# A 192-byte pad under the gate and up weight parts, and another order of the row blocks in the last output-projection column

## The chip, the core and the metric

One NeuronCore of a Trainium2 chip runs the whole kernel. The metric is the device time of one execution in microseconds (us). Between engines the kernel is told by these names: PE is TensorE's matmul stream and PEld its weight loads, DVE is VectorE, ACT is ScalarE, POOL is GpSimd, SP is SyncE, which here only issues DMAs.

## What is computed

One layer of a hybrid block on 512 positions of width 2048, all in float32, and a final RMSNorm:

```python
h = rmsnorm(x, norm1_gain[l])
proj = h @ w_in[l]
o_a = hgrn2_mixer(q_a, f_a, i_a, g_a, lb_all[l], hgrn_norm_gain[l])
o_b = fox_mixer(q_b, k_b, v_b, f_b, fox_gate_bias[l])
x = x + jnp.concatenate([o_a, o_b], axis=-1) @ w_out[l]
h = rmsnorm(x, norm2_gain[l])
x = x + conv_ffn(h, w_ffn_gate[l], w_ffn_up[l], ffn_conv_w[l], ffn_conv_b[l], w_ffn_down[l])
return rmsnorm(x, final_norm_gain)
```

`conv_ffn` multiplies `h` by a gate and an up matrix of 2048 x 5632, passes the gate branch through a causal convolution of width 3 and SiLU, multiplies it with the up branch, and projects back to 2048.

## The kernel before

**Products in parts.** Every float32 product is made of three float32r matmuls: each operand is split into a high part (an ACT copy to float32r) and a low part (a DVE subtraction), and high x high, low x high and high x low are added up in PSUM. That is lines 218 to 220 for the projections and lines 850 to 852 for gate and up.

**Stages.** The input projections, the two mixers, the output projection (columns `d` of 128, each a sum over 16 row blocks `k`, lines 763 to 770), gate and up together (44 blocks `f` in `glu`, line 861), the down projection, the final norm. In the output projection a tile `os_[k]` holds the two parts of row block `k` of the mixers' output, two tiles of 2048 bytes per partition each, in the pool `pa`. All 16 columns read all 16 blocks; the last column (`d` = 15) reads them in the order `LASTK` (line 768), and the host lays its weights out in that order (line 1058).

**The gate and up stage.** The two matrices of a block `f` go through a fast scheme of seven products of half size (`ORDER`, line 785, `NAMES`, line 705) instead of eight. The weights arrive from HBM in tiles `wq` of 4096 bytes per partition (pool `wf`, eight of them, lines 788 to 797), SP issues the loads and POOL those that add to a tile while they land. ACT and DVE split each into `fhi` and `flo` (pool `wh`, four of each, lines 832 to 835). A product is 8 x 3 matmuls with the weight part as stationary operand and a 128x256 piece of the normalised activations (the forms `b11`, `n1`, `b21`, `n2`, `b22`, `n4`, `t3`) as moving operand; 44 x 7 x 24 = 7392 matmuls.

**The passage between them.** After the last column `pa` and the weight stream's pools are closed, and `wf` and `wh` open on the same SBUF bytes (lines 771 to 784), and `tl`, which takes the last pieces of the forms. A new tile waits for the last reader of each old tile under it, tile by tile, so a `wq` load waits for the matmul of the last column that reads the row block that lies below it. The last column's result goes through `x1_out` (lines 747 to 761): DVE adds the rows of x that POOL loaded into `xr` (line 749, 750), SP stores the sum (line 751), ACT squares it and scales it into `hg` (lines 245, 754), and ACT and DVE make the last pieces of the forms (lines 716 to 719). A scheduler sets the order of each engine's instructions when the program is built, not the order of the lines: on ACT the first `fhi` (line 834) stands behind the square, `hg` and three forms of the last column.

**The pad.** `shifted(SHIFT)` (lines 73 and 783) takes a tile of `SHIFT` float32 per partition between `wf` and `wh`. All that is allocated above it moves with it: `fhi`, `flo`, and the tiles of `glu` (pool `gt`, line 902). By the addresses of the built program the forms begin at multiples of 512 bytes, and so do the weight parts of the projections; `fhi` and `flo` begin 64 bytes past one.

Of the kernel before, what the change touches and what calls it, by code (L numbers as in the profile page):

```python
# [25 lines left out]
SCALE = 128.0**-0.5  # L26
NEG = -1.0e30
RAW = 1024
LASTK = (4, 5, 3, 6, 0, 1, 7, 2, 8, 9, 10, 11, 12, 13, 14, 15)
PIECE = 512  # L30
NLATE = 4
ND = KT - NLATE
# [7 lines left out]
KP = KT // 2  # L40
FORM = KP * P
LEAD = 2
SHIFT = 16
EVEN = 376
EVEN_CM = 24
EVEN_SM = 40
# [11 lines left out]
def tile_hymba_block(ctx: ExitStack, tc: tile.TileContext, xT, wst, wgu, wdn, wfb, consts, out, out_t):  # L58
# [5 lines left out]
    def opened(name, bufs, side="left", **kw):  # L64
        cm = tc.tile_pool(name=name, bufs=bufs, side=side, reuse_waits="tile", **kw)
        pools[name] = (cm, cm.__enter__())
        return pools[name][1]
# [5 lines left out]
    def shifted(n):  # L73

        opened("sh", 1).tile([P, n], F32, name="shift")
# [28 lines left out]
    def MM():  # L104
        return mm.tile([P, T], F32, name="mmt", tag="mm")
# [116 lines left out]
    def unit(ps, ks, hs, first=True, last=True):  # L222

        for i, k in enumerate(ks):
            mms(ps, [(k, *ws.block())], hs, first and i == 0, last and i == len(ks) - 1)
            step()
# [539 lines left out]
    for d in range(WOPEN, KT):  # L766
        ps = MM()
        unit(ps, range(KT) if d < KT - 1 else LASTK, os_)
        if d < KT - 1:
# [12 lines left out]
    wf = opened("wf", 8)  # L782
    shifted(SHIFT)
    wh = opened("wh", LEAD + 2)
# [252 lines left out]
def _weights(w_in, w_out, w_gate, w_up, w_down):  # L1037
# [3 lines left out]
    def cols(w, c0, n):  # L1041
        return w[:, c0:c0 + n].reshape(-1, P, n).transpose(1, 0, 2).reshape(P, -1)
# [14 lines left out]
    parts += [cols(w_out, d * P, P) for d in range(WOPEN, KT - 1)]  # L1057
    order = np.concatenate([np.arange(k * P, (k + 1) * P) for k in LASTK])
    parts.append(cols(w_out[order], last, P))
# [50 lines left out]
```

## Time and profile before

| | |
|---|---|
| median of 3 runs | 2238.32 us |
| lowest and highest | 2236.76 and 2239.03 us |
| profiled execution | 2237.23 us |
| its span, first to last instruction | 2235.5 us |
| time around the span | 1.73 us |
| PE busy | 2217.3 us, 99% of the span, 13662 matmuls |
| PEld, DVE, ACT, POOL busy | 1975.1, 1449.0, 947.3, 148.2 us |
| mean granted TensorE clock | 0.997 of full |

A row of the timeline gives the start in us from the span's start, the duration, engine, line, operation, tiles as out<-in, shape, and in brackets how long the engine stood idle before it and what ended that. Equal neighbours are merged into one row with their count. Matmuls are pipelined: the duration of one is longer than the distance from its start to the next one's, and it is the distance that adds up to time.

### The profile page before, as it was taken

How to read it: one execution, taken by the hardware profiler on the slowest of the kernel's cores; microseconds unless marked ns; L12 is line 12 of the kernel's file. 1: busy time of each engine (PE TensorE's matmuls, PEld its weight loads, DVE VectorE, ACT ScalarE, POOL GpSimd, SP SyncE). 2: the span in 40 equal slices, each digit the busy share in tenths (PEclk: the TensorE clock that was granted, in tenths of full speed). 3: DMA queues.
4: the chain of work that ended last, by engine and by line, in shares of the span. 5: the costliest groups of instructions: out<-in, count | busy, mean ns of one | idle time of the engine just before them, and what ended most of it. 6: DMA issues, size and time to landing. Idle time of an engine off the chain costs nothing.

```text
span 2235.5 us, 34427 instructions
## 1 busy us (share of the span) xinstructions
PE 2217.3 (99%) x13662; PEld 1975.1 (88%) x13662; DVE 1449.0 (65%) x2210; ACT 947.3 (42%) x1528; POOL 148.2 (7%) x243
## 2 busy tenths in 40 slices
PE   9999999999999999999999999999999999999998
PEld 8888888788888887999999999999999888888886
DVE  6666467646457464888888888888888433333345
ACT  6333233234335454555555555555555222222334
POOL 0000000000000000100000000000002402010000
PEclk9999999999999999999999999999999999999999
DMA  5222322222222354788888888888887935242233
GB/s 192 85 76 86 99 71 98 76 85 76 87 83 78 125 162 145 230 222 219 222 226 227 220 223 224 224 220 218 223 221 201 377 114 199 94 172 101 87 102 113
DMA packets 112066, 352.14 MB, mean 158 GB/s; under 512 B 12800, under 2 KB 19072, under 8 KB 111904
## 3 DMA queue, kind: packets, MB, share of 16 engines
q1 hardware_dynamic: 89568, 272.67, 36.4%
q0 software_dynamic: 22192, 77.15, 15.5%
q8 instruction: 107, 1.75, 0.3%
q14 instruction: 55, 0.45, 0.1%
q10 hardware_dynamic: 144, 0.12, 0.0%
HBM read 318.43 MB, written 31.46 MB: 157 GB/s over the span
## 4 chain that ended last, share of the span: by engine, by line
PE 98%; DMA 1%; DVE 1%; ACT 0%; issue 0%; DVEq 0%; POOL 0%; ACTq 0%; POOLq 0%
PE pq L850 12%; PE pq L852 12%; PE pq L851 12%; PE mmt L218 9%; PE mmt L220 9%; PE mmt L219 9%; PE mxt L218 7%; PE mxt L219 7%; PE mxt L220 7%; PE mmt L300 3%; PE mmt L302 3%; PE mmt L301 3%; DMA raw<-wdn 0%; PE mxt L452 0%; PE mxt L643 0%; PE mxt L1028 0%
## 5 line engine op out<-in xcount | busy, mean ns | idle before, releaser
L164 DVE TENSOR_TENSOR wlo<-raw,whi 128x512 fp32r<-128x512 f32 x453 | 311.7, 689 | 447.7 <-ACT whi L163 406.6
L163 ACT ACTIVATE whi<-raw 128x512 fp32r<-128x512 f32 x453 | 284.6, 630 | 664.8 <-PE mxt L219 300.4
L835 DVE TENSOR_TENSOR flo<-wq,fhi 128x1024 fp32r<-128x1024 f32 x308 | 376.1, 1222 | 93.4 <-ACT fhi L834 89.7
L834 ACT ACTIVATE fhi<-wq 128x1024 fp32r<-128x1024 f32 x308 | 326.2, 1060 | 236.7 <-issue 105.4
L218 PE MATMUL mmt<-at,whi 128*128 128x512 f32 x896 | 354.7, 396 | 0.0
L220 PE MATMUL mmt<-at,wlo 128*128 128x512 f32 x896 | 349.7, 390 | 0.0
L219 PE MATMUL mmt<-at,whi 128*128 128x512 f32 x896 | 349.3, 390 | 0.0
L218 PE MATMUL mxt<-qt,whi 128*128 128x512 f32 x660 | 256.1, 391 | 1.0 <-ACT whi L163 0.9
L220 PE MATMUL mxt<-qt,wlo 128*128 128x512 f32 x660 | 256.8, 389 | 0.0
L219 PE MATMUL mxt<-qt,whi 128*128 128x512 f32 x660 | 256.5, 389 | 0.0
L220 PEld LDWEIGHTS mmt<-at,wlo 128*128 128x128 f32 x896 | 168.2, 188 | 36.0
L218 PEld LDWEIGHTS mmt<-at,whi 128*128 128x128 f32 x896 | 168.3, 188 | 34.5 <-issue 1.9
L219 PEld LDWEIGHTS mmt<-at,whi 128*128 128x128 f32 x896 | 168.4, 188 | 33.0
L218 PEld LDWEIGHTS mxt<-qt,whi 128*128 128x128 f32 x660 | 123.9, 188 | 27.4 <-ACT whi L163 1.7
L220 PEld LDWEIGHTS mxt<-qt,wlo 128*128 128x128 f32 x660 | 123.9, 188 | 25.9
L219 PEld LDWEIGHTS mxt<-qt,whi 128*128 128x128 f32 x660 | 123.9, 188 | 25.5 <-issue 0.2
L797 POOL DMA_DIRECT2D wq<-wgu x87 | 75.0, 862 | 754.2 <-DMA wq<-wgu 316.3
L818 DVE TENSOR_TENSOR wq<-wq 128x1024 f32<-128x1024 f32 x88 | 107.6, 1222 | 1.5
L850 PE MATMUL pq<-b11h,fhi 128*128 128x256 f32 x352 | 98.3, 279 | 4.1 <-ACT fhi L834 4.1
L300 PE MATMUL mmt<-whi,at 128*128 128x512 f32 x256 | 100.8, 394 | 0.0
L850 PE MATMUL pq<-b21h,fhi 128*128 128x256 f32 x352 | 97.8, 278 | 2.1 <-ACT p L869 2.1
L301 PE MATMUL mmt<-whi,at 128*128 128x512 f32 x256 | 99.7, 390 | 0.0
(304 smaller groups left out, 5033.1 us busy)
## 6 DMA issues: line engine op xcount, KB each, us to landing
wq<-wgu SPq DMA_DIRECT2D x220, 512.0 KB, 5.7
raw<-wst SPq DMA_DIRECT2D x143, 512.0 KB, 3.4
wq<-wgu POOLq DMA_DIRECT2D x87, 512.0 KB, 7.8
raw<-wdn SPq DMA_DIRECT2D x87, 512.0 KB, 3.5
qt<-actd POOLq DMA_DIRECT2D x88, 256.0 KB, 6.9
actd<-ah SPq DMA_DIRECT2D x44, 256.0 KB, 2.9
actd<-al SPq DMA_DIRECT2D x44, 256.0 KB, 5.3
xt<-xT SPq DMA_DIRECT2D x16, 256.0 KB, 5.8
```

The lines of the kernel that those rows point to most:

```text
L163: queue_ends[:] = [s.activation(hi, src, AF.Copy), v.tensor_tensor(lo, src, f32(hi), op=ALU.subtract)]
L164: v.tensor_tensor(lo, src, f32(hi), op=ALU.subtract)]
L218: pe.matmul(ps, lhsT=a, rhs=xh[:, ts], start=(first and i == 0), stop=False)
L219: pe.matmul(ps, lhsT=a, rhs=xl[:, ts], start=False, stop=False)
L220: last_mm[:] = [pe.matmul(ps, lhsT=b, rhs=xh[:, ts], start=False, stop=(last and i == n - 1))]
L300: pe.matmul(pss[i], lhsT=xh[:, ts], rhs=hi, start=(k == 0), stop=False)
L301: pe.matmul(pss[i], lhsT=xl[:, ts], rhs=hi, start=False, stop=False)
L834: s.activation(hi, t, AF.Copy)
L835: v.tensor_tensor(lo, t, f32(hi), op=ALU.subtract)
L850: pe.matmul(ps, lhsT=a, rhs=th, start=(first and j == 0), stop=False, **kw)
L851: pe.matmul(ps, lhsT=a, rhs=tl, start=False, stop=False, **kw)
L852: last_mm[:] = [pe.matmul(ps, lhsT=b, rhs=th, start=False, stop=(j == KP - 1), **kw)]
```

## The change

Two constants are changed and nothing else.

```diff
-LASTK = (4, 5, 3, 6, 0, 1, 7, 2, 8, 9, 10, 11, 12, 13, 14, 15)
+LASTK = (11, 12, 4, 5, 6, 3, 7, 0, 1, 8, 2, 9, 10, 13, 14, 15)
-SHIFT = 16
+SHIFT = 48
```

`SHIFT` counts float32, so the pad grows from 64 to 192 bytes per partition; `fhi`, `flo` and the tiles of `glu` lie 128 bytes higher, and the first `fhi` begins 192 instead of 64 bytes past a multiple of 512. No instruction is added or taken away.

**PE, the last column of the output projection.** `mmt` is the column's sum in PSUM, `whi` and `wlo` the weight parts, and each three rows are one row block: `at_6007` and `at_6008` are the parts of block 11, `at_6014` and `at_6015` those of block 12, `at_5924` and `at_5925` those of block 4.

```order
 L219 MATMUL mmt_7391<-at_6303,whi_7410 128x512
 L220 MATMUL mmt_7391<-at_6302,wlo_7411 128x512
+L218 MATMUL mmt_7469<-at_6007,whi_7428 128x512
+L219 MATMUL mmt_7469<-at_6008,whi_7428 128x512
+L220 MATMUL mmt_7469<-at_6007,wlo_7429 128x512
+L218 MATMUL mmt_7469<-at_6014,whi_7428 128x512
+L219 MATMUL mmt_7469<-at_6015,whi_7428 128x512
+L220 MATMUL mmt_7469<-at_6014,wlo_7429 128x512
 L218 MATMUL mmt_7469<-at_5924,whi_7428 128x512
 L219 MATMUL mmt_7469<-at_5925,whi_7428 128x512
```

Blocks 11 and 12 were the twelfth and thirteenth of the column and are the first two now: 11 blocks, or 33 matmuls, earlier.

**SP, the first loads of the gate and up weights.** `wq` are the eight tiles, `x1d` is the store of column 14's sum; in brackets stand the semaphores that a load waits for, PE_49 being that of the matmuls.

```order
 L751 DMA x1d<-xr 128x512 [waits DMAHW0_49,DVE_49]
+L795 DMA wq<-wgu 128x1024 [waits PE_49] x2
+L795 DMA wq<-wgu 128x1024 [waits DMAHW3_49,PE_49]
 L795 DMA wq<-wgu 128x1024 [waits PE_49]
-L795 DMA wq<-wgu 128x1024
-L795 DMA wq<-wgu 128x1024 [waits DMAHW3_49]
-L795 DMA wq<-wgu 128x1024
-L795 DMA wq<-wgu 128x1024 [waits DMAHW5_49]
-L795 DMA wq<-wgu 128x1024 [waits DMAHW6_49]
-L795 DMA wq<-wgu 128x1024 [waits DMAHW7_49]
-L795 DMA wq<-wgu 128x1024 [waits DMAHW0_49]
```

Before, the first load waited for the matmul of line 219 on block 12, the 38th of the column's 48, and the other seven had nothing of PE left to wait for. Now each of the eight waits for PE by itself: in their order for the 5th, 11th, 14th, 20th, 29th, 35th, 38th and 39th matmul of the column.

**ACT, the passage.** Its order is the same in both programs; this is that of the changed one, from the square of column 15 on.

```order
L245 ACTIVATE sq<-xr 128x512 [waits DVE_49]
L754 ACTIVATE hg<-xr,con 128x512
L717 ACTIVATE b21h_7598<-hg 128x256 [waits Activation_49]
L717 ACTIVATE b22h_7608<-hg 128x256
L717 ACTIVATE n2h_7604<-tq 128x256 [waits DVE_49]
L834 ACTIVATE fhi<-wq 128x1024 [waits DMAHW1_49]
```

The first `fhi` stands behind the five operations of column 15, as before. One wait ahead of these rows has another value: `b11h` of the last pair of columns (line 717) waits for a matmul that stands nine later than before. DVE's order is the same in both programs too.

## Rows read from the trace of the kernel before

**Rows 1.** The page: busy time by engine, and the chain that ended last.

```profile
PE 2217.3 (99%) x13662; PEld 1975.1 (88%) x13662; DVE 1449.0 (65%) x2210; ACT 947.3 (42%) x1528; POOL 148.2 (7%) x243
...
PE 98%; DMA 1%; DVE 1%; ACT 0%; issue 0%; DVEq 0%; POOL 0%; ACTq 0%; POOLq 0%
```

**Rows 2.** Waits of PE: for whom, us in total, times, longest.

```profile
PE pq L850 <- ACT fhi L834: 4.1, 1, 4.1
...
PE pq L850 <- ACT p L869: 2.1, 1, 2.1
...
PE pq L852 <- DVE flo L835: 0.6, 1, 0.6
```

**Rows 3.** Timeline of PE, end of the last column and after.

```profile
887.18 0.39 PE L219 MATMUL mmt<-at,whi 128*128 128x512 f32 x1
...
889.45 0.39 PE L220 MATMUL mmt<-at,wlo 128*128 128x512 f32 x1
893.90 0.58 PE L850 MATMUL pq<-b11h,fhi 128*128 128x256 f32 x1 [4.06 <-ACT fhi L834]
...
899.91 0.28 PE L850 MATMUL pq<-n1h,fhi 128*128 128x256 f32 x1
...
905.44 0.28 PE L852 MATMUL pq<-n2h,flo 128*128 128x256 f32 x1
```

**Rows 4.** Timeline of SP, POOL, DVE and ACT in the passage.

```profile
869.44 0.33 SPq L156 DMA_DIRECT2D raw<-wst  x1
...
879.72 0.33 SPq L751 DMA_DIRECT2D x1d<-xr  x1
...
882.23 0.42 ACT L717 ACTIVATE b11h<-hg 128x256 fp32r<-128x256 f32 x1 [1.26 <-PE mmt L219]
...
882.24 0.54 POOL L749 DMA_DIRECT2D xr<-xT  x1 [10.20 <-DMA x1d<-xr]
...
887.61 12.18 SPq L795 DMA_DIRECT2D wq<-wgu  x9
...
889.88 0.69 DVE L750 TENSOR_TENSOR xr<-xr,mmt 128x512 f32<-128x512 f32 x1 [8.45 <-PE mmt L220]
...
890.60 0.63 ACT L245 ACTIVATE sq<-xr 128x512 f32<-128x512 f32 x1 [0.31 <-DVE xr L750]
...
892.50 0.40 ACT L717 ACTIVATE n2h<-tq 128x256 fp32r<-128x256 f32 x1
892.81 1.04 ACT L834 ACTIVATE fhi<-wq 128x1024 fp32r<-128x1024 f32 x1
...
895.48 0.42 DVE L718 TENSOR_TENSOR t3l<-tq,t3h 128x256 fp32r<-128x256 f32 x1
895.81 1.22 DVE L830 TENSOR_TENSOR wq<-wq 128x1024 f32<-128x1024 f32 x1
```

**Rows 5.** DMA issues at 887.6, 882.2, 871.5 and 899.3 us: size, us to landing.

```profile
wq<-wgu SPq DMA_DIRECT2D x1, 512.0 KB, 3.6
xr<-xT POOLq DMA_DIRECT2D x1, 256.0 KB, 3.1
xr<-xT POOLq DMA_DIRECT2D x1, 256.0 KB, 3.3
wq<-wgu POOLq DMA_DIRECT2D x1, 512.0 KB, 9.4
```

**Rows 6.** Timeline of ACT before PE's second wait.

```profile
905.69 1.06 ACT L834 ACTIVATE fhi<-wq 128x1024 fp32r<-128x1024 f32 x1 [0.61 <-ACT fhi L834]
906.77 1.28 ACT L263 ACT_TABLE_LOAD   x1
908.06 0.20 ACT L263 ACTIVATE sd<-va 128x4 f32<-128x4 f32 x1
908.17 0.37 ACT L869 ACTIVATE p<-pq 128x256 f32<-128x256 f32 x1
```

**Rows 7.** Stretches: start:end, length, PE busy (matmuls), granted clock, DMA share, GB/s.

```profile
892.70:899.60 6.90, 5.11 (x22) 0.51 1.07 406
909.90:913.20 3.30, 3.30 (x18) 0.50 1.02 371
1000.00:1700.00 700.00, 700.00 (x6179) 1.00 0.82 221
```

**Rows 8.** Timeline of PE in the stretch from 909.9 us on.

```profile
910.05 0.41 PE L852 MATMUL pq<-b21h,flo 128*128 128x256 f32 x1
...
912.83 0.41 PE L850 MATMUL pq<-b22h,fhi 128*128 128x256 f32 x1
```

## The prediction

> **What bounds the kernel now.** I read the page first: PE is busy for 2217.3 of 2235.5 us and the chain that ended last runs through PE for 98% of the span [rows 1]. So only two things can move the time: PE's few idle stretches, and the distance from one matmul to the next. The waits of PE are the next view. All of them over half a microsecond in the two stages that the change touches are three: 4.1 us and 0.6 us at the start of the gate and up stage, where the first product waits for `fhi` and then for `flo`, and 2.1 us two products later, for ACT's copy of a sum [rows 2]. From then on the stage runs without a wait; 6179 matmuls in 700.0 us are 0.1133 us from one to the next [rows 7]. The last look is at the passage itself, engine by engine, to see who holds PE there.
>
> PE's last matmul of the output projection starts at 889.45 and ends at 889.84, and the first of the next stage starts at 893.90 [rows 3]. In between DVE adds column 15 to x (889.88), ACT squares the sum (890.60) and goes through `hg` and three forms without a break to 892.50, and the first `fhi` starts at 892.81 [rows 4]. The reader is to see what is missing in that last row: there is no bracket. `fhi` did not wait for its weights; ACT came to it straight from `n2h`. Its load was issued at 887.61 [rows 4] and landed 3.6 us later [rows 5], at 891.2, which is 1.6 us before ACT was free. The same holds for the second product: DVE adds `a22` to `s1` at 895.81, straight after `t3l` [rows 4].
>
> **The new order of row blocks.** No matmul is added, and PE's order inside the column changes nothing for PE, because all 16 blocks are long there. What moves is SP's loads. The matmul that the first load waited for starts at 887.18 [rows 3], and 33 matmuls earlier at 0.227 us each ((889.45 - 887.18) / 10 [rows 3]) makes 7.5 us: the load goes out at about 880.1, right behind the store of column 14 at 879.72 [rows 4]. By the positions in the column the others follow at 881.5, 882.2, 883.5, 885.6, 886.9, 887.6 and 887.8. The first tile lands at about 883.7 instead of 891.2. But the wait that ends last at 893.90 is ACT's, and ACT's order is unchanged: `fhi` still stands behind `n2h`, that behind DVE's sum, and that behind PE's last matmul. Gain: 0. What lies beside the loads is ACT's own chain from 889.88 to 892.81; it covers them now by 1.6 us and after the change by 9 us.
>
> One wait moves the other way: ACT's `b11h`, which started at 882.23 [rows 4], waits for a matmul nine later, 9 x 0.227 = 2.0 us. Behind it on ACT stands only what started at 889.88 and later, so this is hidden by 5 us. Cost: 0.
>
> The second wait does not depend on the loads either. ACT starts an `fhi` at 905.69, 0.25 us after PE started the last matmul of the product before (905.44 [rows 3]), loads a table for 1.28 us, takes a root and copies the sum for 0.37 us [rows 6], and PE goes on. I put the start of that `fhi` down to PE, which still reads the buffer that it writes; the view names ACT's own `fhi` there, which can't be it. Gain: 0.
>
> What could be lost is the row load `xr` for column 15. It starts at 882.24 on POOL, once the store of column 14 has landed, and takes 3.1 us [rows 4, 5], so it lands at 885.3, 4.5 us before DVE needs it at 889.88. Now the first `wq` loads are under way beside it. Nearest row: the same load one column earlier, 2 us behind a 512 KB weight load that SP issued at 869.44, took 3.3 us [rows 4, 5]. Far row: a POOL load behind SP's full queue took 9.4 us [rows 5], and it is twice as large. With 3.3 nothing happens; with 9.4 `xr` would land at 891.6 and the passage would be 1.8 us longer. The loads come at 0.7 to 2.0 us from each other and not eight at once, so I take the near row: cost 0, with 0 to 1.8 us as bounds. A rule speaks against the change here: the Trainium skill (DMA: Bandwidth & Descriptors, Issuing engines are not separate DMA queues) says that DMAs of all issuing engines run on the same 16 engines and interleave. The 9.4 us agree with it, the 3.3 us say how little one neighbour costs. By the rule alone the cost would be the 1.8 us.
>
> **The pad.** `fhi` and `flo` move by 128 bytes. On ACT and DVE that touches no wait of PE after the passage. On PE it could change the distance between matmuls, if weight load and moving operand get in each other's way by their addresses; no row shows a pad of 192. From below: at half the clock the distance is (912.83 - 910.05) / 13 = 0.2138 us [rows 8], half of that is 0.1069, so at full clock 0.0064 us per matmul are something else; were it the pad's, 7392 x 0.0064 = 47 us could go. From above: the 48 matmuls from 899.91 to 905.44 stand (905.44 - 899.91) / 47 = 0.1177 us apart [rows 3], at the same pad; were this the rule in the stage, it would cost 7392 x 0.0044 = 33 us. I take 0. The output projection, whose weight parts have no pad at all, needs 0.227 us for 512 columns [rows 3], and the padded stage 0.1133 for 256 [rows 7]: the same per column, so two placements give one pace, and a third should too.
>
> **The sum** is 0, against the profiled execution's 2237.23 us (span 2235.5 and 1.73 around it). The median of the three runs is 1.1 us above it; carried over, the forecast is **2238.3 us**. A measurement of this kernel tells about 0.2%, 4.5 us, from no change.
>
> **The rivals.**
>
> *The loads were the bound after all (faster, 2231.0 us).* If something in `fhi`'s start hung on the loads, the whole start could go: 4.06 us of wait, and the first product, whose 24 matmuls took 899.91 - 893.90 = 6.0 us [rows 3] for want of `flo` and at a granted clock of 0.51, the lower of its two levels (1.2 GHz), to which it fell while PE stood still [rows 7], where 24 x 0.1133 = 2.7 are due. That is 4.06 + 3.3 = 7.3 us. For it: PE stands still just there, and the loads are what the change moves. Against it: the missing bracket, and 1.6 us of slack. The Trainium skill (DMA: Bandwidth & Descriptors, Rules for kernel authors) says to issue a DMA early, compute, and wait for it late; by that this rival is what one expects, but here the trace has the wait on ACT. 14%.
>
> *The pad costs pace (slower, 2271 us).* The weight reads then fall against the moving operand's so that the slow distance of 0.1177 us becomes the stage's own: +33 us. If only one of the three matmuls of a step suffers it is 11 us, 2249. It decides from 0.0006 us per matmul on (4.5 / 7392). For it: the slow distance exists. Against: it came once, after the first product, and the same buffers run at 0.1133 later. 11%.
>
> *The row load comes late (up to 1.8 us, 2240.1; or more).* The wait grows from 4.06 to 5.9 us, and a longer wait can lengthen the stretch at half the clock, where 18 matmuls took 3.3 us instead of 2.0 [rows 7], 1.3 us each: 1.8 + 2 x 1.3 = 4.4 us with two, and more with a third. 8%, of which 5 lie within 0.2%.
>
> *The pad gains pace (faster, 2191 us).* The 47 us from above. Against it stands the equal pace per column. 5%.
>
> **How the numbers follow.** The forecast has 62%. Within 0.2% lie it and five of the third rival: 0.67. Faster are the first and the last: 0.19. Slower are the second and three of the third: 0.14. The range reaches down to the first rival's 2231 and up over the late row load to 2243; it leaves out both results of the pad, 16%.
>
> **What would show it.** In the changed kernel's timeline SP's first `wq` load stands near 880.1 and the eight are spread to 887.8; `fhi` again starts about 2.9 us after the last matmul's end, with no wait for a DMA; PE waits 4.1, 0.6 and 2.1 us in the same three places; the stretch from 1000 to 1700 us holds 6179 matmuls again, give or take two. A bracket with a DMA at DVE's addition of column 15 would be the third rival. The forecast is wrong if PE's first wait shrinks by more than a microsecond, or if the distance in the long stretch leaves 0.1133.

## The result and the profile after

The changed kernel takes 2269.12 us (median of 4 runs, 2268.60 to 2269.88) against 2238.24 us before (4 runs): 1.0139 times as long, 95% interval 1.0126 to 1.0151. The forecast was 2238.3 us, the range ended at 2243; the rival "the pad costs pace" had 2271. The profiled execution took 2269.88 us, with a span of 2268.2.

PE's waits first, as [rows 2] shows them for before:

```profile
PE pq L850 <- ACT fhi L834: 4.1, 1, 4.1
PE mxt L1017 <- DVE dg L1010: 3.2, 1, 3.2
PE pq L850 <- ACT p L869: 2.1, 1, 2.1
...
PE pq L852 <- DVE flo L835: 0.6, 1, 0.6
```

In the passage and the stage behind it nothing waits longer. The passage, in the order of [rows 4], from the timelines of SP, POOL, DVE and ACT of the changed kernel:

```profile
879.80 0.33 SPq L751 DMA_DIRECT2D x1d<-xr  x1
880.21 19.66 SPq L795 DMA_DIRECT2D wq<-wgu  x9
...
882.47 0.54 POOL L749 DMA_DIRECT2D xr<-xT  x1 [10.33 <-DMA x1d<-xr]
...
884.35 0.42 ACT L717 ACTIVATE b11h<-hg 128x256 fp32r<-128x256 f32 x1 [3.30 <-PE mmt L219]
...
889.96 0.69 DVE L750 TENSOR_TENSOR xr<-xr,mmt 128x512 f32<-128x512 f32 x1 [8.45 <-PE mmt L220]
...
892.58 0.40 ACT L717 ACTIVATE n2h<-tq 128x256 fp32r<-128x256 f32 x1
892.89 1.04 ACT L834 ACTIVATE fhi<-wq 128x1024 fp32r<-128x1024 f32 x1
```

The first load goes out 7.4 us earlier, and `fhi` starts again where ACT is done with `n2h`: 892.89 instead of 892.81. The whole passage stands 0.08 us later, as the column before it already does (the store at 879.80 instead of 879.72), and is no longer and no shorter.

The long stretch is where the time is. The stretches of [rows 7], of the changed kernel (start:end, length, PE busy with its matmuls, granted clock, DMA share, GB/s):

```profile
892.70:899.60 6.90, 5.03 (x25) 0.56 0.98 208
909.90:913.20 3.30, 3.30 (x21) 0.62 0.93 227
1000.00:1700.00 700.00, 700.00 (x5946) 1.00 0.79 213
```

PE is busy for all of the 700 us, at the full clock (2.4 GHz), with 5946 matmuls instead of 6179. That is 0.1177 us from one to the next instead of 0.1133; by their starts, 7272 matmuls from 915.90 to 1772.66, it is 0.1178, the value that the text uses. The last matmul of the stage starts at 1772.66 us instead of 1740.70; less the 0.08 us, that is 31.9 us of the 32.7 by which the span grew. No wait of PE shows any of it; only the count in a stretch does.

The changed kernel also held the fast pace for a while. PE's timeline, from the second product on:

```profile
899.58 0.28 PE L850 MATMUL pq<-n1h,fhi 128*128 128x256 f32 x1
...
905.12 0.28 PE L852 MATMUL pq<-n2h,flo 128*128 128x256 f32 x1
...
908.26 0.39 PE L850 MATMUL pq<-b21h,fhi 128*128 128x256 f32 x1 [2.08 <-ACT p L869]
...
912.49 0.28 PE L851 MATMUL pq<-b21l,fhi 128*128 128x256 f32 x1
...
915.10 0.28 PE L850 MATMUL pq<-b22h,fhi 128*128 128x256 f32 x1
...
915.44 1.02 PE L277 MATMUL mxt<-dg,ones 128*128 128x512 f32 x2
915.90 0.68 PE L850 MATMUL pq<-n4h,fhi 128*128 128x256 f32 x1
```

From 899.58 to 905.12 are 47 distances, 0.1179 us each, and from 912.49 to 915.10 are 23, 0.1135 us each; then comes a float32 matmul of the norm (line 277), and behind it the pace is 0.1178 to the end of the stage. Between the first two stretches lie eight small matmuls of the norm, the wait of 2.1 us, and a stretch at half the clock (1.2 GHz), which began when PE had been going again for 0.7 us:

```profile
909.00:912.40 3.40, 3.40 (x19) 0.50 0.90 263
```

The kernel before does the same up to the matmul of line 277. It has 0.1177 us at first [rows 3], and then

```profile
913.96 0.28 PE L852 MATMUL pq<-b22h,flo 128*128 128x256 f32 x1
...
915.66 0.28 PE L852 MATMUL pq<-b22h,flo 128*128 128x256 f32 x1
915.78 1.02 PE L277 MATMUL mxt<-dg,ones 128*128 128x512 f32 x2
```

15 distances of 0.1133 us. Only behind that matmul do the two kernels part: the one before keeps 0.1133 to the end of the stage, the changed one falls back.

### The profile page after: what moved, and what is told of

Read it like the earlier page. It is cut to its first block, busy times and chain, and to the rows that moved or that the text cites. A ratio compares the mean times of both kernels' runs of the same rounds, so it can differ in the third digit from the quotient of the medians.

```text
span 2268.2 us, 34432 instructions
## 1 busy us (share of the span) xinstructions
PE 2249.1 (99%) x13662; PEld 2006.8 (88%) x13662; DVE 1451.7 (64%) x2210; ACT 950.6 (42%) x1528; POOL 148.3 (7%) x243
## 4 chain that ended last, share of the span: by engine, by line
PE 98%; DMA 1%; DVE 1%; ACT 0%; issue 0%; SPq 0%; DVEq 0%
PE pq L851 13%; PE pq L850 13%; PE pq L852 13%; PE mmt L218 9%; PE mmt L220 9%; PE mmt L219 9%; PE mxt L219 7%; PE mxt L218 7%; PE mxt L220 7%; PE mmt L300 3%; PE mmt L302 2%; PE mmt L301 2%; DMA raw<-wdn 1%; PE mxt L452 0%; PE mxt L643 0%; PE mxt L1028 0%
```

## The experiments

### Which of the two edits

```diff
-SHIFT = 16
+SHIFT = 48
```

> The pad of 192 bytes with the old order of row blocks. Theory A, the pad alone sets the distance between matmuls of the gate and up stage: 0.1178 us through the stage, 2269 us. Theory B, the stage has a fast and a slow pace at any pad, and what happens in the passage (with the new order the half-clock stretches begin 0.9 us earlier) leaves PE in one of them: with the old order the pace is 0.1133 us and the time 2238 us. Theory C, it takes both: 2238 us here and in the run with the order alone.

Measured: 2269.91 us, ratio 1.0145 (1.013 to 1.016), and again 5946 matmuls from 1000 to 1700 us.

```diff
-LASTK = (4, 5, 3, 6, 0, 1, 7, 2, 8, 9, 10, 11, 12, 13, 14, 15)
+LASTK = (11, 12, 4, 5, 6, 3, 7, 0, 1, 8, 2, 9, 10, 13, 14, 15)
```

> The new order of row blocks with the pad of 64 bytes. Theory A: the pace is 0.1133 us, 2238 us, and PE's three waits stay at 4.1, 0.6 and 2.1 us. Theory B: 0.1178 us and 2269 us. Theory C: 2238 us.

Measured: 2237.13 us (10 runs) against 2237.10 (13), ratio 1.0000 (0.9990 to 1.0009), 6179 matmuls. The pad alone gives the whole loss, and the order of the row blocks nothing, as forecast for it. Theories B and C fall as they were put. Both paces occur at either pad, as theory B said, but the order of the row blocks does not choose between them.

### Other pads

No pad (the pool opens without its tile), and `SHIFT` of 32, 8, 12, 24 and 80 (the first two of these edits are shown), each with the old order:

```diff
-    shifted(SHIFT)
+    opened("sh", 1)
```

> Old order, no pad at all: the first weight part begins at a multiple of 512 bytes, as the forms do. Theory A needs one pace for this place and can't say which; by the old projections, whose parts lie at multiples of 512 and run at the same pace per column as the stage with 64 bytes, it is 0.1133 us and 2238 us. Theory B: the timing of the passage is that of before, so 0.1133 us and 2238 us whatever the pad.

```diff
-SHIFT = 16
+SHIFT = 32
```

> Old order, a pad of 128 bytes, between the two. Theory A: one of the two paces through the whole stage, 2238 or 2269 us; if the place within 128 bytes counts, 64 and 192 would have been alike, so a slow pace here would say that larger distances are bad and a fast one that 192 is a place by itself. Theory B: 0.1133 us and 2238 us whatever the pad.

> Old order, pad of 32 bytes, between 0 (0.1200 us) and 64 (0.1133 us). If a step of 64 bytes has to be crossed, the pace is that of no pad, 0.1200 us and 2285 us; if the pace falls with the distance, about 0.1167 us and 2261 us; if any distance of 32 will do, 0.1133 us and 2238 us.

> Old order, pad of 48 bytes. If the pace falls evenly from 32 to 64, 0.1158 us and about 2256 us; if 64 is a narrow place, about 0.118 us and 2272 us; if a good stretch reaches down here, 0.1133 us and 2238 us. A pace under 0.1133 us would say that 17 sixteenths of the columns are no floor.

> Old order, pad of 96 bytes. So far the pace goes by the distance of the weight part from the form, taken modulo 256 bytes: 0 gives 0.1200 us, 32 0.1183, 64 and 320 0.1133, 128 0.1187, 192 0.1178. If 64 is the middle of a good stretch, 96 keeps 0.1133 us and 2238 us; if 64 is a narrow place, it lies near the value of 128: 0.1187 us and 2276 us.

> Old order, pad of 320 bytes, which is 64 more than 256. If places 256 bytes apart are alike, 0.1133 us and 2238 us. If they are alike only 512 bytes apart, or the distance itself counts, another pace, between 0.1133 and 0.1200 us, up to 2286 us.

Measured, with the matmuls that each profile has from 1000 to 1700 us:

| pad, bytes | matmuls in 700 us | us each | time, us | ratio to before |
|---|---|---|---|---|
| 0 | 5836 | 0.1200 | 2285.41 | 1.0215 (1.0195 to 1.0236) |
| 32 | 5918 | 0.1183 | 2273.17 | 1.0158 (1.0137 to 1.0178) |
| 48 | 6178 | 0.1133 | 2237.85 | 0.9997 (0.9986 to 1.0009) |
| 64 | 6179 | 0.1133 | (before) | 1 |
| 96 | 5901 | 0.1186 | 2271.11 | 1.0143 (1.0093 to 1.0192) |
| 128 | 5902 | 0.1186 | 2276.26 | 1.0174 (1.0154 to 1.0195) |
| 192 | 5946 | 0.1177 | 2269.91 | 1.0145 (1.0130 to 1.0160) |
| 320 | 6179 | 0.1133 | 2237.44 | 0.9999 (0.9989 to 1.0009) |

It is no slope: 48 and 64 are good, 32 and 96 are not. 320 is as good as 64, which fits a repeat after 256 bytes. The pad of 96 has two times 9 us apart, 2275.73 us, the profiled one, and 2266.50. No pad gains anything over 64.

The run with 320 shows both paces, too. Ahead of the norm's matmul it has

```profile
911.11 0.28 PE L850 MATMUL pq<-b21h,fhi 128*128 128x256 f32 x1
...
915.24 0.28 PE L852 MATMUL pq<-b22h,flo 128*128 128x256 f32 x1
```

which are 35 distances of 0.1180 us, and behind it the 0.1133 of the table. So the table tells which pace the stage is left in behind that matmul, and not the only pace that a pad can have.

### Is it the place, or the distance between the two operands?

The forms are moved down by 128 bytes and the weight parts stay at 64, so the distance is 192:

```diff
-SHIFT = 16
-EVEN = 376
+SHIFT = 48
+EVEN = 248
...
+    opened("shr", 1, "right").tile([P, 32], F32, name="shiftr")
     tt = opened("tt", 1, "right")
...
     tl = opened("tl", 1)
+    tl.tile([P, 96], F32, name="shiftl")
...
```

(`SHIFT` gives back here what the tile in `tl` moves `wh` by, up to a multiple of 512; the tiles of `glu` keep their places in the same way, and `wq` moves with the forms.)

> Old order, weight parts at 64 bytes past a multiple of 512 as before, but the forms, the moving operand, 128 bytes lower, so that the weight part lies 192 bytes past the form's place. If the distance between the two operands counts, the pace is that of the pad of 192: 0.1178 us and about 2269 us. If the weight part's own place counts (or its place against DVE, ACT or the tiles of the gated unit), it is that of the pad of 64: 0.1133 us and 2238 us.

Measured: 2281.62 us, and in the long stretch

```profile
1000.00:1700.00 700.00, 700.00 (x5946) 1.00 0.77 212
```

the same count as with the pad of 192, to the matmul. So the weight part's own place does not settle the pace: it stands where it stood before, and both runs are slow. The place of the moving operand counts as well, and the distance between the two is the simplest reading; one such move does not prove it. That the count is the same says little by itself, for 64 bytes turn out below to have the very same slow pace. The other 12 us over the forecast lie behind the stage: there PE waits for the down projection's first weight parts, 4.5 us in all (1.5 in the changed kernel), and the granted clock is 0.50 from 1776.2 to 1782.9 us. Why was not followed up.

### Does the pad pay, or cost, in the projections?

```diff
-EVEN = 376
+EVEN = 248
...
     wr = opened("wr", 2)
+    opened("shw", 1).tile([P, 16], F32, name="shiftw")
     wp = opened("wp", 4)
...
     wr = opened("wr", 3)
+    opened("shw", 1).tile([P, 16], F32, name="shiftw")
     wp = opened("wp", 4)
...
```

The run with 128 bytes has `[P, 32]` in both places.

> Old order, pad of 64 bytes as before, and the same pad of 64 bytes under the weight parts of the projections and the down projection as well (512 bytes are taken from the unused room at the other end, which moves nothing against multiples of 512). Theory F, the 17 sixteenths of 512 and 256 columns are what the moving operand takes by itself: 0.2267 us between their matmuls as before, 2237 us. Theory G, a weight load at the same place as the moving operand costs 0.0067 us at any width, as it does without a pad at 256 columns (0.1200 - 0.1133): 0.2200 us, 4668 matmuls x 0.0067 = 31 us less, 2206 us. Theory H, the pad hurts at 512 columns: slower.

> As the run with 64 bytes under the projections' weight parts, but with 128. There 512 columns took 0.2333 us instead of 0.2267 and the kernel 2267 us. Theory K, at 512 columns a distance of 0 is the good place and every other costs: 0.229 to 0.234 us, 2250 to 2275 us. Theory L, the good place for 512 columns is somewhere else and 0 is only one of those at the floor: 0.2267 us or less, 2238 us or less.

Measured: 2266.76 us with 64 bytes and 2266.07 with 128 (ratios 1.0131 and 1.0120, intervals 1.0114 to 1.0148 and 1.0091 to 1.0149). The gate and up stage kept 6179 matmuls in its 700 us. In the down projection, the stretch from 1800 to 2000 us of before, of the run with 64 and of that with 128:

```profile
1800.00:2000.00 200.00, 200.00 (x884) 1.00 0.43 147
```

```profile
1800.00:2000.00 200.00, 200.00 (x859) 1.00 0.37 133
```

```profile
1800.00:2000.00 200.00, 200.00 (x862) 1.00 0.38 135
```

Counted by the distances, one fewer than the matmuls, that is 0.2265, 0.2331 and 0.2323 us. At 512 columns a distance of 0 is good and 64 is bad; at 256 columns it is the reverse. Theories F, G and L fall, H and K stand: the good place of one width is not that of the other. Whether 512 columns have two paces at one distance, too, was not tried.

### The distance, or the break before the stretch?

The two paces at one pad, seen above, asked for a run that puts a break into the stream. In the changed kernel one more float32 matmul stands in each of 43 blocks; nobody reads its result:

```diff
         product(g + 3, y)
+        if f:
+            pe.matmul(MX()[:, 0:P], lhsT=ones, rhs=ident, start=True, stop=True)
```

> The changed kernel with one more float32 matmul of 128 columns in each of 43 blocks of the gate and up stage, whose result nobody reads (some 0.25 us each, 11 us in all). In the changed kernel the pace was 0.1133 us for 23 matmuls, until a float32 matmul stood in between, and 0.1178 us from then to the stage's end. Theory M, the distance of 192 bytes fixes the pace after any such break: 0.1178 us throughout, about 2280 us. Theory N, the pace is an accident of the last break and lasts to the next: blocks of both paces, 2250 to 2280 us.

Measured: 2269.19 us. Six stretches of 18 us, each between two such matmuls:

```profile
934.00:952.00 18.00, 18.00 (x161) 1.00 0.77 208
953.50:971.50 18.00, 18.00 (x155) 1.00 0.76 197
973.50:991.50 18.00, 18.00 (x155) 1.00 0.74 194
993.50:1011.50 18.00, 18.00 (x161) 1.00 0.78 213
1012.70:1030.70 18.00, 18.00 (x156) 1.00 0.78 210
1032.70:1050.70 18.00, 18.00 (x156) 1.00 0.73 196
```

One good (161 matmuls, by their starts 0.1133 us), two bad (155 or 156, 0.1178 us), one good, two bad: the turn holds through all 43 blocks. Theory N has it, though not as an accident: the paces come in a fixed order. In these blocks the pace is what the last break leaves, and it stays until the next.

Then the same matmuls at 64 bytes and at none, and a single one in the changed kernel (`if f == 1`):

> The kernel before (pad of 64 bytes) with one more float32 matmul of 128 columns in each of 43 blocks. With 192 bytes the stretches between two such matmuls ran in a fixed turn, one at 0.1133 us and two at 0.1178. Theory P, the turn belongs to the matmul stream and the pad only shifts which break lands where: the same turn here, about 2258 us. Theory Q, at 64 bytes every phase is good: 0.1133 us in all stretches, about 2245 us. Theory R, at 64 bytes two phases of three are good: two stretches at 0.1133 and one slower.

> The kernel without a pad, with the same 43 matmuls. Without them it held 0.1200 us and 2285 us. Theory P: a turn with one stretch in three at 0.1133 us, about 2270 us. Theory S, at distance 0 there is no good phase: 0.1200 us in all stretches, about 2292 us.

> The changed kernel, pad of 192 bytes and all, with that matmul in the second block alone; with one in each block the stretch behind the first one ran at 0.1133 us. If the pace is what the last break leaves and stays to the next, the stage runs at 0.1133 us to its end and the change's whole loss is gone: 2238 to 2239 us. If 192 bytes pull the pace down again after a while, more, up to 2269 us.

Measured at 64 bytes: 2264.30 us, ratio 1.0119 (1.0098 to 1.0141). Its first four stretches:

```profile
933.00:951.00 18.00, 18.00 (x155) 1.00 0.77 209
952.80:970.80 18.00, 18.00 (x161) 1.00 0.78 206
972.20:990.20 18.00, 18.00 (x155) 1.00 0.77 208
992.20:1010.20 18.00, 18.00 (x161) 1.00 0.80 209
```

Bad and good in turn, to the end of the stage, so 64 bytes have a bad pace too, and it is that of 192. None of the three theories had a turn of two. Without a pad 2293.75 us, and in such stretches 152 or 153 matmuls, fewer than in the bad ones here; no good pace was seen, which is theory S. Three of them:

```profile
935.00:953.00 18.00, 18.00 (x153) 1.00 0.72 191
955.30:973.30 18.00, 18.00 (x152) 1.00 0.74 198
975.70:993.70 18.00, 18.00 (x152) 1.00 0.69 189
```

With one matmul in the second block and the pad left at 192, six runs took 2240.36, 2268.46, 2269.75, 2269.44, 2239.98 and 2269.66 us: one and the same kernel, two times some 29 us apart. (Its median of 2268.95 and ratio of 1.0141 say little.) The profiled execution is the first, 2240.36 us; before the added matmul, at 933.3 us, and behind it:

```profile
917.00:932.00 15.00, 15.00 (x129) 1.00 0.48 149
935.00:950.00 15.00, 15.00 (x135) 1.00 0.69 193
1000.00:1700.00 700.00, 700.00 (x6178) 1.00 0.81 222
```

129 matmuls in 15 us, then 135, and to the end the count of the kernel before: one matmul turned the bad pace into the good one for the rest of the stage, with both operands where they were. In four of six runs, by their times, it did not. The added matmul also shifts by one the PSUM buffers that some later products write; as one kernel has both times, that does not decide the pace.

## Why the prediction was wrong

**The order of the row blocks: right, step by step.** The first load was put at 880.1 us and went out at 880.21; PE's three waits kept their 4.1, 0.6 and 2.1 us; the order alone measures 1.0000. The missing bracket at `fhi` was the right thing to read: a transfer that ends 7 us earlier gains nothing where its reader isn't free. The rival that the loads were the bound is out.

**The row load: harmless, but sized too low.** I took the 3.3 us of the near row. It took

```profile
xr<-xT POOLq DMA_DIRECT2D x1, 256.0 KB, 5.5
```

in the changed kernel (issued at 882.47, landed at 888.0), 2 us before DVE needed it. Beside the loads it took 2.4 us longer than the 3.1 us of before [rows 5], and the slack covered that. The prediction's rule of the Trainium skill (DMA: Bandwidth & Descriptors, Issuing engines are not separate DMA queues), that DMAs of all issuing engines share the same 16 engines and interleave, agrees with the 2.4 us.

**The pad: wrong, and here the forecast fell.** The step was "I take 0 ... the same per column, so two placements give one pace, and a third should too". The two placements belonged to two widths. At 256 columns no row of before showed a distance other than 64, and at 512 none other than 0; I read one good place for each as a proof that the place doesn't matter. The runs show that it does for both, and that the good places differ. The term set to 0 measured 31.9 us. The price of the rival was right: 33 us (0.0044 us x 7392). That it fits so well is in part luck: it was read off the slow pace of 64 bytes, which turned out to be that of 192 as well, while the pad of 128 cost 39 us and no pad 48 us.

**The sign that I explained away.** Against that rival I wrote that the slow distance "came once, after the first product, and the same buffers run at 0.1133 later". Both were true, and they were the warning: one set of addresses with two paces means that the addresses alone don't fix the pace. 48 matmuls at 0.1177 us were in the trace of before, at the very pace that the change made the rule, and I had nothing that explained why they stopped.

**What is shown and what is open.** Shown: the pad makes the loss; the loss lies in the distance from one matmul to the next and in no wait; the place of the weight part alone does not settle it, since moving the moving operand brings the loss as well; the pace is also a matter of the last break in the matmul stream, and one break can undo the loss with the pad left alone. Argued, not shown: that it is the distance between the two operands of PE that counts. In the streams as they are, 64 bytes ended in the good pace in all 41 runs of before that stood beside the experiments (2236.22 to 2240.13 us), and 192 in the bad one in all 8 of the change and of the pad alone. Why a break ends in this pace or that, and what inside the chip meets at these places, stays open. The Trainium skill (TensorE: Matmul & The Clock Gate, Step-by-step: what each phase is for) says that loading the next weights takes no read bandwidth from the running matmul, since each has its own read port. By that one would not expect the placement to matter; here, with the same instructions at other addresses, the stage ended at paces from 0.1133 to 0.1200 us at 256 columns. No run shows that it is the reading of the weights that costs this.

No version beats the kernel before: 48 and 320 bytes and the order alone equal it within 0.1%. The pad of 192 is not worth taking, and the new order costs nothing and buys nothing.

## What to carry to other kernels

When a stage is bound by PE, a pad or a moved pool can be an edit of the inner loop: price it as a change of the distance between two matmuls times their number, and don't call it free because no engine waits for it. Two paces with the operands at the same places say that the loop can settle in either; the count of matmuls in equal stretches shows it, the waits don't. Tune such a pad on the chip for each width by itself, and try it again after any edit that puts another matmul into the stream.

## What the runs showed of the chip that I had not expected

- The pace in which a stream of float32r matmuls settles depends on where weight part and moving operand lie: at 256 columns 0.1133 us with the weight part 48, 64 and 320 bytes past the moving operand's place modulo 512, 0.1183 at 32, 0.1186 at 96 and 128, 0.1178 at 192 and 0.1200 at 0. At 64, 192 and 320 both 0.1133 and 0.1178 were seen.
- At 512 columns a distance of 0 runs at 0.2265 us, 64 and 128 at 0.233 and 0.232.
- The pace outlives its cause: after one foreign matmul it held for over 700 us. With a break in each block it went in a fixed turn, one of three blocks good at 192 bytes, one of two at 64, none at 0.
